# Mixture-of-experts stages: weight rows in 8 KB runs, and the gather of the next pair moved into the current pair

## The chip, the cores and the metric

The kernel runs on one core of a Trainium2 chip. The time is that of one execution on the device, in microseconds (us); the profile is of one such execution. PE is the matrix engine and PEld its loads of the stationary operand; DVE, ACT and POOL are the other compute engines, and SP issues nearly all weight transfers. SBUF is the memory on the core, with 128 partitions, and PSUM holds the sums of PE.

## The reference

A stack of layers on 256 tokens of 1024 features, all in f32. Two of them end in a mixture of 32 experts, and the change concerns these two stages alone:

```python
def moe(x):                                   # x [256, 1024]
    g = softmax(x @ w_rg + b_rg)              # 4 groups, the best one is taken
    e = softmax((x @ w_re + b_re)[group])     # 8 experts in it, the best two
    gates = g_best * e_best / sum(e_best)
    for each expert e, for its tokens xb:
        h = silu(xb @ w_gate[e]) * (xb @ w_up[e])     # [1024, 512] each
        y[tokens] += gate * (h @ w_down[e])           # [512, 1024]
    return y
x = layer_norm(ALPHA * x + moe(x))
```

Every expert is computed in 64 places, whether or not so many tokens chose it; an expert with more tokens is continued in a loop at run time (`more`), which the inputs at hand may leave empty.

## The kernel before

`moe` (L1281 and below) handles the 32 experts as 16 pairs. In a pair, 128 rows of the products are the 64 places of the one expert and the 64 of the other, and PE computes both side by side.

- **Router.** Logits are summed over the eight feature chunks of `X["h"]` and `X["l"]` (L1302, L1303), as the layer norm before it delivers them. DVE finds groups, experts and places. `xt` is x with tokens on partitions, made by 16 transposes.
- **Gather.** `ot` is a 0/1 matrix (tokens by places) for a pair. `xg` is `xt` transposed times `ot`: 16 products (L1455) whose stationary operand is a block of 128 features of `xt`. Each f32 product is two loads and two multiplies on PE, so 32 steps. The results stand in two PSUM tiles of the pool `mp` (tag "m", two buffers, which `ogp`, `htp` and both `yp` use as well, in the order of the code) and are copied to SBUF (L1460).
- **Weights of the places.** `ogt` is `ot` times the gates; it is transposed into `ogp` (L1463) and copied to `og` on ACT.
- **Gate and up.** 64 products into `gps` and `ups` (L1478).
- **Activation.** ACT takes the tanh (L188); DVE makes `t` (L1493, L1494); PE transposes it in four blocks, `htp` (L1497); DVE copies it to `hT` (L1499).
- **Down.** 32 products into two `yp` (L1510), which ACT copies to `y` (L1519). `y` shares one SBUF buffer with `xg` (tag "xy").
- **Combine.** Eight products of `y` and `og` add to the sums `eacc` (L1535). Before pair 0 combines, `residual` (L1437) puts x times ALPHA into these sums, with 16 products of `xt`.

The last pair (`last`) also computes means and high and low parts for the layer norm that follows.

Weights come through `load`: per expert two tiles each of gate, up and down, 1 MiB each, into a ring of 21 tiles (`ORDER`: rooms of several pools) that `next_tile` takes in turn. SP runs ahead of PE; a transfer waits until its tile is free. The rows of a matrix are spread over partitions by

```python
w[k][h * 512:(h + 1) * 512, :].rearrange("(c p) m -> p c m", p=128)   # gate, up: 4 runs of 2 KB a partition
w[2][h * 256:(h + 1) * 256, :].rearrange("(c p) m -> p c m", p=128)   # down: 2 runs of 4 KB a partition
```

`more()` stands behind pair `MOREQ` = 10. Its loop body, which also takes tiles of the ring, is in a branch on a count that DVE computes after pair 1 (`beyond`).

The order of the instructions on an engine is largely that of the code, but the program that builds the kernel may move an instruction that is ready ahead of one that waits. `warm` puts idle products on PE behind an instruction.

Of the kernel before, what the change touches and what calls it, by code (L numbers as in the profile page):

```python
# [10 lines left out]
F32 = mybir.dt.float32  # L11
# [7 lines left out]
D = 1024  # L19
S = 256  # L20
# [11 lines left out]
W1 = 0  # L32
# [15 lines left out]
def tile_stack(ctx: ExitStack, tc: tile.TileContext, a: dict, out: bass.AP):  # L48
# [20 lines left out]
    def after_norm(*ins):  # L69
        """no split but the first few between the operations of a layer norm."""  # L70
# [21 lines left out]
    def project_group(tiles, ws):  # L92
        """up to four chunks at once, (wh, wl, width) each; features outermost, so that it can start on the first."""
        for c in range(KC):
            for i, (wh, wl, n) in enumerate(ws):
                mm3(tiles[i // 2][0:n, i % 2, :], wh[:, c], wl[:, c], X["h"][:, c, :], X["l"][:, c, :],
                    first=(c == 0 and i % 2 == 0), last=(c == KC - 1), skip=True)
        return [tiles[i // 2][:, i % 2, :] for i in range(len(ws))]
# [74 lines left out]
    X = {}  # L173

    def x_tile(key, shape=(128, KC, S), dtype=F32R):
        """the room of a part of x; between its last reader and the next x it takes weights."""
# [13 lines left out]
    def table(name):  # L190
        """the functions' tables, loaded behind the last tanh."""
# [4 lines left out]
    def warm(out, n, after):  # L196
        """the array's clock falls in a pause: idle products, into a sum not in use, keep it up."""
# [5 lines left out]
    def last_chunks(accs, ks, first):  # L203
        """the products of the last chunks, (wh, wl, mh, ml) each, into one output chunk."""
# [7 lines left out]
    def finish(accs, last, scale, g, b, write=None, loaded=False, mean=None, side="right"):  # L212
        """last(c) makes output chunk c of the sum in accs complete; then x = LN(x * ALPHA + acc / scale),
        or LN(acc) where the sum has x in it and its mean is known.

        The variance is taken about the mean of the first
        eighth of the features: the shift from the true mean is at most a few deviations, so the correction
        loses nothing."""
# [99 lines left out]
    def ffn(l, w1, w2, g, b, setup=None):  # L318
        with pool(name="accps", bufs=1, space=PSUM) as aps, pool(name="gups", bufs=2, space=PSUM) as gps, \
# [26 lines left out]
            def gate_up(js):  # L346
                """the hidden chunks js; features outermost, so that it can start on the first of them."""
# [42 lines left out]
    def log1p_exp_neg_abs(pool, x, shape, tag):  # L390
        """log(1 + exp(-|x|)) by the series of atanh."""
# [34 lines left out]
    def bias_tile(pool, h, queue=None, bufs=3):  # L426
        """T[q, k] = rel[bucket(128 + q - k), h], with the mask of the head's kind."""
# [48 lines left out]
    def token_mix(l):  # L476
        w_in, w_gate, w_out = a["w_in"][l], a["w_gate"][l], a["w_out"][l]
        with ExitStack() as st:
# [25 lines left out]
            def split_pair(t0, t1, c0):  # L504
                """stationary columns: 64 of t0, 64 of t1."""
# [19 lines left out]
            def k_pad(ps, kz, i):  # L525
                """a projected pair of keys into two tiles, each with zeros in the other's rows."""
# [10 lines left out]
            def v_tok(ps, v, i):  # L537
                """keys on partitions: v[:, tile, i, :]."""
# [7 lines left out]
            # compressed keys and values  # L546
# [28 lines left out]
            def compress(i, ts):  # L575
                """four products side by side, then their sum."""
# [26 lines left out]
            # compressed keys  # L603
# [23 lines left out]
            # compressed values  # L627
# [15 lines left out]
            # gates of the three branches and the forget gate  # L643
# [15 lines left out]
            # the running sums of the forget gates  # L659
# [9 lines left out]
            # attention over the compressed blocks, all heads at once  # L669
# [29 lines left out]
            def attend(q, kz, bias, sink=None, gate=None):  # L699
                """probabilities of one head, keys on partitions: [k0 x (q0 q1) | k1 x q1]."""  # L700
# [27 lines left out]
            def pv(po, jobs):  # L728
                """jobs[g]: list of (v of tile 0, v of tile 1 or None, probabilities)."""
# [55 lines left out]
            # NSA  # L785
# [17 lines left out]
            # sliding window with sinks  # L803
# [20 lines left out]
            # forgetting attention  # L824
# [79 lines left out]
    def rsqrt_tile(pool, v, eps, n=S):  # L904
        """(v + eps) ** -0.5, refined by a step of Newton's."""
# [9 lines left out]
    def ssd(g, b):  # L915
        w_in, w_out = a["ssd_w_in_2"][0], a["ssd_w_out_2"][0]
        with ExitStack() as st:
# [13 lines left out]
            def conv(ps, c, dst):  # L931
                """causal convolution of four taps, then twice its silu."""
# [9 lines left out]
            # the keys and queries of the states, B and C  # L942
# [6 lines left out]
            # steps, decays and their running sums  # L949
# [47 lines left out]
            def mix(j, xs, csb, y):  # L997
                """the states' sums for two heads."""
# [85 lines left out]
    def dilated(g_, b_):  # L1084
        wq, wo = a["attn_w_qkv_2"][0], a["attn_w_o_2"][0]
        with ExitStack() as st:
# [27 lines left out]
            # sin, with its sign by row, and cos, one where nothing turns  # L1114
# [136 lines left out]
    NE, CAP, HID, NOV = 32, 64, 512, 7  # L1251
    AHEAD = 7
    MOREQ = 10
# [18 lines left out]
    def router_parts(rp, l):  # L1272
        """the router's weights, high and low parts side by side."""
# [5 lines left out]
    def moe(l, g_, b_, rs, write=False):  # L1279
        w_g, w_u, w_d = a["moe_w_gate_2"][l], a["moe_w_up_2"][l], a["moe_w_down_2"][l]  # L1280
        with ExitStack() as st:  # L1281
# [17 lines left out]
            # router  # L1299
            ps = mp.tile([72, S], F32, tag="m", name="lgp")  # L1300
            for c in range(KC):
                nc.tensor.matmul(out=ps, lhsT=rs[:, c, :], rhs=X["h"][:, c, :], start=(c == 0), stop=False, skip_group_check=True)  # L1302
                nc.tensor.matmul(out=ps[0:36], lhsT=rs[:, c, 0:36], rhs=X["l"][:, c, :], start=False, stop=(c == KC - 1), skip_group_check=True)  # L1303
            lf = T([72, S], "lf")
# [4 lines left out]
            warm(accs[0][:, 0, :], W1, x)  # L1309
            # the groups' logits, filled up to eight, then the experts'  # L1310
# [7 lines left out]
            def top(x, name):  # L1318
                """the eight highest logits in order, and where they stand."""
# [8 lines left out]
            # the experts of the other groups far below  # L1328
# [8 lines left out]
            # which experts  # L1337
# [5 lines left out]
            # tokens on partitions  # L1343
# [8 lines left out]
            # the place of each token in its expert's list, -1 if it is in none  # L1352
# [7 lines left out]
            warm(accs[0][:, 0, :], W2, x)  # L1360
# [6 lines left out]
            def weights():  # L1367
                """of the experts chosen."""
# [27 lines left out]
            def beyond():  # L1396
                """blocks of 64 places beyond an expert's first"""
# [33 lines left out]
            def residual():  # L1431
# [296 lines left out]
```

## Time and profile before

| | us |
|---|---|
| median of three runs | 2939.56 |
| lowest and highest | 2938.95, 2942.76 |
| span of the profiled execution, first to last instruction | 2939.3 |
| PE busy | 2802.7 (95%) |
| PE loads busy | 2199.8 (75%) |
| DVE busy | 1421.7 (48%) |
| ACT busy | 1050.9 (36%) |
| POOL busy | 196.5 (7%) |

The profile states no other time of its own for the profiled execution than its span. Shares of busy time are means over stages with different limits: a change in one stage is to be read from that stage. A wait is put down to what ended last before the engine went on. PE's products are pipelined, so that the duration of one contains its drain, and the distance between the starts of two is what one costs in a row of them. The first expert stage lies at about 1700 to 2195 us of the span, the second at about 2425 to 2920.

### The profile page before, as it was taken

The page shows a single profiled execution, that of the slowest core. Times are in us where ns is not written, and L with a number is a line of the kernel's source. Part 1 is how long each engine was busy: PE and PEld are TensorE (multiplying, and loading weights), DVE is VectorE, ACT ScalarE, POOL GpSimd, SP SyncE. Part 2 cuts the span into 40 slices and gives each one's busy share as a digit, 9 for nine tenths or more (in the row PEclk, how much of TensorE's full clock was granted, in tenths as well). Part 3 has the DMA queues.
Part 4 walks back from the last instruction along what each step waited for, and adds up shares of the span by engine and source line. Part 5 has one row for each costly group of instructions (what it writes and reads, how often), then busy time and mean ns, then how long its engine had stood idle before and what let it go on. Part 6 is the DMA issues. An engine that isn't in the chain of part 4 may idle for free. (4 is left out here: it accounts for less than half of the span.)

```text
span 2939.3 us, 46679 instructions
## 1 busy us (share of the span) xinstructions
PE 2802.7 (95%) x19161; PEld 2199.8 (75%) x19161; DVE 1421.7 (48%) x3075; ACT 1050.9 (36%) x1949; POOL 196.5 (7%) x263
## 2 busy tenths in 40 slices
PE   8899999999999999999999999999998989999998
PEld 8798899999999889999989854454448974444454
DVE  5466665755655765665688731111127762111113
ACT  4344555544544454544477510000015530000002
POOL 2102000200201100020100100000001010000000
PEclk9899999999999999999999999999999999999999
DMA  8666454455454745445455699998985479999896
GB/s 223 193 201 158 126 159 138 156 184 185 149 194 137 186 130 167 153 139 193 131 194 180 229 364 393 395 393 323 393 305 169 137 256 356 394 393 393 300 394 230
DMA packets 426793, 697.44 MB, mean 237 GB/s; under 512 B 19460, under 2 KB 238384, under 8 KB 426576
## 3 DMA queue, kind: packets, MB, share of 16 engines
q1 hardware_dynamic: 414976, 677.62, 66.3%
q10 hardware_dynamic: 9296, 11.66, 1.3%
q0 software_dynamic: 2304, 5.15, 1.2%
q8 instruction: 152, 2.49, 0.4%
q14 instruction: 65, 0.53, 0.1%
HBM read 693.25 MB, written 4.27 MB: 237 GB/s over the span
## 5 line engine op out<-in xcount | busy, mean ns | idle before, releaser
L84 DVE TENSOR_TENSOR whl<-w,whl 128x1024 fp32r<-128x1024 f32 x487 | 591.5, 1220 | 349.2 <-ACT whl L83 344.2
L83 ACT ACTIVATE whl<-w 128x1024 fp32r<-128x1024 f32 x487 | 507.3, 1050 | 355.9 <-PE gu L113 105.8
L111 PE MATMUL pp<-xh,whl 128*128 128x256 f32 x1432 | 418.1, 292 | 9.0 <-ACT xh L307 4.0
L112 PE MATMUL pp<-xl,whl 128*128 128x256 f32 x1432 | 418.7, 292 | 1.0 <-DVE xl L308 1.0
L113 PE MATMUL pp<-xh,whl 128*128 128x256 f32 x1432 | 412.8, 288 | 0.4 <-DVE whl L510 0.4
L111 PE MATMUL gu<-xh,whl 128*128 128x256 f32 x1408 | 401.6, 286 | 9.9 <-DVE h L361 7.2
L113 PE MATMUL gu<-xh,whl 128*128 128x256 f32 x1408 | 401.4, 285 | 0.5 <-DVE whl L84 0.5
L112 PE MATMUL gu<-xl,whl 128*128 128x256 f32 x1408 | 401.6, 285 | 0.0
L111 PEld LDWEIGHTS pp<-xh,whl 128*128 128x128 f32 x1432 | 274.6, 192 | 17.4 <-ACT xh L307 5.7
L112 PEld LDWEIGHTS pp<-xl,whl 128*128 128x128 f32 x1432 | 275.0, 192 | 10.0 <-issue 6.9
L111 PEld LDWEIGHTS gu<-xh,whl 128*128 128x128 f32 x1408 | 272.8, 194 | 12.2 <-ACT whl L83 9.4
L113 PEld LDWEIGHTS pp<-xh,whl 128*128 128x128 f32 x1432 | 274.6, 192 | 4.3 <-issue 2.4
L112 PEld LDWEIGHTS gu<-xl,whl 128*128 128x128 f32 x1408 | 273.0, 194 | 0.8 <-DVE xl L308 0.7
L113 PEld LDWEIGHTS gu<-xh,whl 128*128 128x128 f32 x1408 | 272.9, 194 | 0.8 <-DVE whl L84 0.8
L1460 DVE COPY xg<-xgp 128x512 f32<-128x512 f32 x60 | 41.5, 692 | 358.5 <-PE xgp L1455 358.5
L111 PE MATMUL acc<-hhi,whl 128*128 128x256 f32 x704 | 201.7, 287 | 2.4 <-DVE rT L231 2.2
L112 PE MATMUL acc<-hlo,whl 128*128 128x256 f32 x704 | 200.1, 284 | 0.0
L113 PE MATMUL acc<-hhi,whl 128*128 128x256 f32 x704 | 199.1, 284 | 0.0
L1493 DVE SCALAR_TENSOR_TENSOR t<-t,gps 128x512 f32<-128x512 f32 x32 | 22.0, 688 | 324.4 <-ACT t L188 324.4
L1519 ACT ACTIVATE y<-yp 128x512 f32<-128x512 f32 x60 | 35.8, 597 | 347.7 <-PE yp L1510 347.7
L111 PEld LDWEIGHTS acc<-hhi,whl 128*128 128x128 f32 x704 | 135.8, 193 | 5.4 <-DVE rT L231 4.0
L112 PEld LDWEIGHTS acc<-hlo,whl 128*128 128x128 f32 x704 | 135.8, 193 | 0.2
(571 smaller groups left out, 5063.0 us busy)
## 6 DMA issues: line engine op xcount, KB each, us to landing
w<-in_ffn_w_dram SPq DMA_DIRECT2D x130, 1024.0 KB, 5.3
wa<-in_moe_w_up_dram SPq DMA_DIRECT2D x48, 1024.0 KB, 14.2
whl<-in_moe_w_down_dram SPq DMA_DIRECT2D x47, 1024.0 KB, 14.1
wa<-in_moe_w_gate_dram SPq DMA_DIRECT2D x43, 1024.0 KB, 14.2
whl<-in_moe_w_gate_dram SPq DMA_DIRECT2D x39, 1024.0 KB, 14.1
wa<-in_moe_w_down_dram SPq DMA_DIRECT2D x37, 1024.0 KB, 13.4
whl<-in_moe_w_up_dram SPq DMA_DIRECT2D x36, 1024.0 KB, 14.2
w<-in_moe_w_down_dram SPq DMA_DIRECT2D x32, 1024.0 KB, 14.4
```

The source lines that it names most:

```text
L83: after_norm(nc.scalar.activation(out=hi, in_=w, func=AF.Copy), nc.vector.tensor_tensor(out=lo, in0=w, in1=hi.bitcast(F32), op=ALU.subtract))
L84: nc.vector.tensor_tensor(out=lo, in0=w, in1=hi.bitcast(F32), op=ALU.subtract))
L111: nc.tensor.matmul(out=o, lhsT=wh, rhs=xh, start=first, stop=False, skip_group_check=skip)
L112: nc.tensor.matmul(out=o, lhsT=wh, rhs=xl, start=False, stop=False, skip_group_check=skip)
L113: return nc.tensor.matmul(out=o, lhsT=wl, rhs=xh, start=False, stop=last, skip_group_check=skip)
L1460: nc.vector.tensor_copy(out=xg[:, q * 4:q * 4 + 4, 0:P], in_=ps[:, :, 0:P])
L1493: nc.vector.scalar_tensor_tensor(out=t[0:P], in0=t[0:P], scalar=1.0, in1=gps[0:P], op0=ALU.add, op1=ALU.mult)
L1519: nc.scalar.activation(out=y[0:P, hs], in_=yp[0:P], func=AF.Copy)
```

## The change

- Weights: row 4p + c of a gate or up tile and row 2p + c of a down tile now go to partition p, so that a partition's part of a tile is one run of 8 KB.
- To match, the gather takes every fourth feature from `xt` as the columns of a stationary operand, and the transposes of `t` take every second one.
- The gather becomes a function of two halves. Pair 0's runs before the pairs; that of pair q + 1 runs within pair q: its first half behind the tanh in the code, its second half behind the copy of `hT`. The first half's copy to `xg` goes to ACT, the second's to DVE. `xg` has a buffer of its own; `y` becomes two halves in the rooms of `t` and `hT`.
- `ogp` and `og` move behind the gather's second half, except in the last pair.
- The residual moves into the router: eight products of `alphas` and `X["T"]`, two chunks behind the router's, the last two behind the transposes of the logits. The idle products behind the places (`warm`) write to another tile.
- `more()` moves behind the loads of the last pair and takes a tile of the ring for its `xg`.

The core of the diff (comments and docstrings that it also empties are left out):

```diff
 
 ps = mp.tile([72, S], F32, tag="m", name="lgp")
+def residual(c):
+    nc.tensor.matmul(out=accs[c // 2][:, c % 2, :], lhsT=alphas, rhs=X["T"][:, c, :], start=(c % 2 == 0), stop=False,
+                     skip_group_check=True)
 for c in range(KC):
     nc.tensor.matmul(out=ps, lhsT=rs[:, c, :], rhs=X["h"][:, c, :], start=(c == 0), stop=False, skip_group_check=True)
     nc.tensor.matmul(out=ps[0:36], lhsT=rs[:, c, 0:36], rhs=X["l"][:, c, :], start=False, stop=(c == KC - 1), skip_group_check=True)
+    if c >= 2:
+        residual(c - 2)
 lf = T([72, S], "lf")
 nc.scalar.activation(out=lf, in_=ps, func=AF.Identity, bias=rb[:, l:l + 1], scale=1.0)
 pt = mp.tile([128, 2, 72], F32, tag="m", name="lgt")
 for i in range(2):
     x = nc.tensor.transpose(pt[:, i, :], lf[:, i * 128:(i + 1) * 128], ident[0:72, 0:72])
-warm(accs[0][:, 0, :], W1, x)
+for c in (KC - 2, KC - 1):
+    residual(c)
 lg = T([128, 2, 40], "lg")
 nc.vector.memset(lg[:, :, 4:8], -3.0e38)
 lo = T([128, 2, 36], "lo")
...
-warm(accs[0][:, 0, :], W2, x)
+warm(gup.tile([128, HID], F32, tag="u", name="idle")[:, 0:256], W2, x)
...
 
-def residual():
-    if "r" not in done:
-        done["r"] = True
-        for c in range(KC):
-            for i in range(2):
-                x = nc.tensor.matmul(out=accs[c // 2][:, c % 2, i * 128:(i + 1) * 128], lhsT=xt[:, i, c * 128:(c + 1) * 128],
-                                     rhs=alphas, start=(c % 2 == 0 and i == 0), stop=False, skip_group_check=True)
-                tc.add_manual_dep(x.ins, done["up"].ins.name, order, reason="gates first")
-
 done = {}
 
 def first_copy(k):
     return nc.vector.tensor_copy if k == 0 else (lambda out, in_: nc.scalar.activation(out=out, in_=in_, func=AF.Copy))
 
-def run(os, ogs, loads, n, last):
+def gather(os, P, xg):
+    def half(q):
+        ps = mp.tile([128, 4, 128], F32, tag="m", name="xgp")
+        first = "r" not in done
+        for c in range(4):
+            for i in range(2):
+                nc.tensor.matmul(out=ps[:, c, 0:P], lhsT=xt[:, i, q * 512 + c:(q + 1) * 512:4], rhs=os[i],
+                                 start=(i == 0), stop=(i == 1))
+            if first:
+                first_copy(c % 2)(out=xg[:, q * 4 + c, 0:P], in_=ps[:, c, 0:P])
+        if not first:
+            first_copy(1 - q)(out=xg[:, q * 4:q * 4 + 4, 0:P], in_=ps[:, :, 0:P])
+    return [lambda q=q: half(q) for q in range(2)]
+def run(xg, ogs, loads, n, last, then=()):
     P = n * CAP
     wg, wu, wd = loads
-    xg = wk.tile([128, KC, 128], F32, tag="xy", name="xg", bufs=1)
-    for q in range(2):
-        ps = mp.tile([128, 4, 128], F32, tag="m", name="xgp")
-        for c in range(4):
-            for i in range(2):
-                nc.tensor.matmul(out=ps[:, c, 0:P], lhsT=xt[:, i, (q * 4 + c) * 128:(q * 4 + c + 1) * 128], rhs=os[i],
-                                 start=(i == 0), stop=(i == 1))
-            if "r" not in done:
-                first_copy(c % 2)(out=xg[:, q * 4 + c, 0:P], in_=ps[:, c, 0:P])
-        if "r" in done:
-            nc.vector.tensor_copy(out=xg[:, q * 4:q * 4 + 4, 0:P], in_=ps[:, :, 0:P])
-    ogp = mp.tile([128, S], F32, tag="m", name="ogp")
-    for i in range(2):
-        nc.tensor.transpose(ogp[0:P, i * 128:(i + 1) * 128], ogs[i], ident)
-    og = wk.tile([128, S], F32R if last else F32, tag="og", name="og", bufs=1)
-    nc.scalar.activation(out=og[0:P], in_=ogp[0:P], func=AF.Copy, scale=0.5)
+    then = list(then)
     if last:
+        ogp = mp.tile([128, S], F32, tag="m", name="ogp")
+        for i in range(2):
+            nc.tensor.transpose(ogp[0:P, i * 128:(i + 1) * 128], ogs[i], ident)
+        og = wk.tile([128, S], F32R, tag="og", name="og", bufs=1)
+        nc.scalar.activation(out=og, in_=ogp, func=AF.Copy, scale=0.5)
         ogl = wk.tile([128, S], F32R, tag="ogl", name="ogl", bufs=1)
         nc.vector.scalar_tensor_tensor(out=ogl, in0=ogp, scalar=0.5, in1=og.bitcast(F32), op0=ALU.mult, op1=ALU.subtract)
         room = big.tile([128, 2, D], F32, tag="xtok", name="room")
...
     tanh(out=t[0:P], in_=gps[0:P], scale=0.5)
+    if then:
+        then.pop(0)()
     if last:
         table("natural_log_exp_and_others")
     nc.vector.scalar_tensor_tensor(out=t[0:P], in0=t[0:P], scalar=1.0, in1=gps[0:P], op0=ALU.add, op1=ALU.mult)
     nc.vector.tensor_tensor(out=t[0:P], in0=t[0:P], in1=ups[0:P], op=ALU.mult)
     ht = mp.tile([128, 4, 128], F32, tag="m", name="htp")
     for c in range(4):
-        nc.tensor.transpose(ht[:, c, 0:P], t[0:P, c * 128:(c + 1) * 128], ident[0:P, 0:P])
+        nc.tensor.transpose(ht[:, c, 0:P], t[0:P, c // 2 * 256 + c % 2:(c // 2 + 1) * 256:2], ident[0:P, 0:P])
     hT = wk.tile([128, 4, 128], F32, tag="hT", name="hT", bufs=1)
     nc.vector.tensor_copy(out=hT[:, :, 0:P], in_=ht[:, :, 0:P])
+    if then:
+        then.pop(0)()
+    if not last:
+        ogp = mp.tile([128, S], F32, tag="m", name="ogp")
+        for i in range(2):
+            nc.tensor.transpose(ogp[0:P, i * 128:(i + 1) * 128], ogs[i], ident)
+        og = wk.tile([128, S], F32, tag="og", name="og", bufs=1)
+        nc.scalar.activation(out=og[0:P], in_=ogp[0:P], func=AF.Copy, scale=0.5)
     yl = None
     if last:
         y, yl = split_tile([128, D])
-    else:
-        y = wk.tile([128, D], F32, tag="xy", name="y", bufs=1)
     yps = [mp.tile([128, 512], F32, tag="m", name="yp") for hf in range(2)]
     for c0 in range(0, 4, 2):
         for hf, yp in enumerate(yps):
...
+    if not last:
+        ys = [wk.tile([128, 512], F32, tag=k, name="y", bufs=1) for k in ("t", "hT")]
     for hf, yp in enumerate(yps):
         hs = slice(hf * 512, (hf + 1) * 512)
-        nc.scalar.activation(out=y[0:P, hs], in_=yp[0:P], func=AF.Copy)
+        nc.scalar.activation(out=y[0:P, hs] if last else ys[hf][0:P], in_=yp[0:P], func=AF.Copy)
         if last:
             nc.vector.tensor_tensor(out=yl[:, hs], in0=yp, in1=y[:, hs].bitcast(F32), op=ALU.subtract)
     if last:
...
-        nc.tensor.matmul(out=accs[c // 2][:, c % 2, :], lhsT=y[0:P, cs], rhs=og[0:P],
+        nc.tensor.matmul(out=accs[c // 2][:, c % 2, :], lhsT=ys[c // 4][0:P, c % 4 * 128:c % 4 * 128 + 128], rhs=og[0:P],
                          start=False, stop=True, skip_group_check=True)
 
     if last:
         return combine, mean
-    residual()
+    done["r"] = True
     for c in range(KC):
         combine(c)
 
...
         for k, dst in ((0, wg), (1, wu)):
             for e, w in enumerate(ws):
                 t = next_tile([128, 4, HID])
-                x = nc.sync.dma_start(out=t, in_=w[k][h * 512:(h + 1) * 512, :].rearrange("(c p) m -> p c m", p=128))
+                x = nc.sync.dma_start(out=t, in_=w[k][h * 512:(h + 1) * 512, :].rearrange("(p c) m -> p c m", p=128))
                 if turn[0] < len(slots) and "early" in behind:
                     tc.add_manual_dep(x.ins, behind["early"].ins.name, order, reason="the weights at hand first")
                 dst[e].append(t)
     for h in range(2):
         for e, w in enumerate(ws):
             t = next_tile([128, 2, D])
-            nc.sync.dma_start(out=t, in_=w[2][h * 256:(h + 1) * 256, :].rearrange("(c p) m -> p c m", p=128))
+            nc.sync.dma_start(out=t, in_=w[2][h * 256:(h + 1) * 256, :].rearrange("(p c) m -> p c m", p=128))
             wd[e].append(t)
     return wg, wu, wd
 
-def pair(q):
-    ld = load([(w_g[e], w_u[e], w_d[e]) for e in (2 * q, 2 * q + 1)])
-    os, ogs = [], []
+def places(q):
+    os = []
     for i in range(2):
         o = wk.tile([128, 2, CAP], F32, tag=f"ot{i}", name="ot")
         nc.vector.tensor_tensor(out=o, in0=iota[:, 0:CAP].unsqueeze(1).to_broadcast([128, 2, CAP]),
                                 in1=rk[:, i, 2 * q:2 * q + 2].unsqueeze(2).to_broadcast([128, 2, CAP]), op=ALU.is_equal)
         os.append(o)
-    if q == 0:
-        weights()
+    return os
+def weighted(q, os):
+    ogs = []
     for i, o in enumerate(os):
         og = wk.tile([128, 2, CAP], F32, tag=f"ogt{i}", name="ogt", bufs=1)
         nc.vector.tensor_tensor(out=og, in0=o, in1=gt[:, i, 2 * q:2 * q + 2].unsqueeze(2).to_broadcast([128, 2, CAP]), op=ALU.mult)
-        os[i] = o.rearrange("p e s -> p (e s)")
         ogs.append(og.rearrange("p e s -> p (e s)"))
-    return run(os, ogs, ld, 2, q == NE // 2 - 1)
+    return ogs
+def gather_pair(os):
+    xg = wk.tile([128, KC, 128], F32, tag="xg", name="xg", bufs=1)
+    return xg, gather([o.rearrange("p e s -> p (e s)") for o in os], 2 * CAP, xg)
 
 def more():
     total = nc.values_load(ib[0:1, 7:8], min_val=0, max_val=NOV)
...
                 ogs.append(og)
-            run(os, ogs, ld, 1, False)
-
-for q in range(NE // 2):
-    last = pair(q)
+            xg = next_tile([128, KC, 256])
+            for f in gather(os, CAP, xg):
+                f()
+            run(xg, ogs, ld, 1, False)
+
+NP = NE // 2
+for q in range(NP):
+    ld = load([(w_g[e], w_u[e], w_d[e]) for e in (2 * q, 2 * q + 1)])
+    if q == 0:
+        os = places(0)
+        weights()
+        xg, steps = gather_pair(os)
+        for f in steps:
+            f()
+    if q == NP - 1:
+        more()
+    ogs = weighted(q, os)
+    steps = ()
+    if q < NP - 1:
+        os = places(q + 1)
+        hold = {}
+
+        def first_half(os=os, hold=hold):
+            hold["xg"], hold["steps"] = gather_pair(os)
+            hold["steps"][0]()
+
+        steps = (first_half, lambda hold=hold: hold["steps"][1]())
+    last = run(xg, ogs, ld, 2, q == NP - 1, steps)
+    if q < NP - 1:
+        xg = hold["xg"]
     if q == 1:
         beyond()
-    if q == MOREQ:
-        more()
 st4.close()
 ocp = st.enter_context(pool(name="oc", bufs=2))
 o = []
 
 def out_chunk(c):
-    """chunk c of x to where it belongs, tokens on partitions."""
+
     if c % 2 == 0:
         o[:] = [ocp.tile([128, 2, 256], F32, tag="oc", name="oc")]
```

## Rows read from the trace of the kernel before

**Rows 1.** the page's slices: GB/s moved in 40 equal slices of the span
```profile
GB/s 223 193 201 158 126 159 138 156 184 185 149 194 137 186 130 167 153 139 193 131 194 180 229 364 393 395 393 323 393 305 169 137 256 356 394 393 393 300 394 230
```

**Rows 2.** stretches: length, busy by engine (instructions), PEclk, DMA share, GB/s
```profile
1816.00:1836.00 20.00, 19.82 (x108) 10.99 (x110) 2.33 (x7) 1.58 (x3) 0.00 (x0) 1.00 1.05 387
...
1838.00:1848.00 10.00, 8.31 (x42) 2.90 (x40) 2.06 (x3) 0.60 (x1) 0.00 (x0) 1.00 1.03 407
...
2007.00:2020.00 13.00, 13.00 (x78) 8.52 (x76) 1.38 (x2) 1.58 (x3) 0.00 (x0) 1.00 0.06 26
```

**Rows 3.** order of time on DVE: start, duration, instruction; the copies of hT
```profile
1721.41 0.69 DVE L1499 COPY hT<-htp 128x512 f32<-128x512 f32 x1 [0.84 <-PE htp L1497]
...
1753.97 0.69 DVE L1499 COPY hT<-htp 128x512 f32<-128x512 f32 x1 [0.81 <-PE htp L1497]
...
2030.72 0.69 DVE L1499 COPY hT<-htp 128x512 f32<-128x512 f32 x1 [0.81 <-PE htp L1497]
...
2062.06 0.69 DVE L1499 COPY hT<-htp 128x512 f32<-128x512 f32 x1 [0.81 <-PE htp L1497]
...
2751.21 0.69 DVE L1499 COPY hT<-htp 128x512 f32<-128x512 f32 x1 [0.81 <-PE htp L1497]
...
2783.95 0.69 DVE L1499 COPY hT<-htp 128x512 f32<-128x512 f32 x1 [0.81 <-PE htp L1497]
```

**Rows 4.** waits of PE's loads, second stage: us in total, times, longest
```profile
PEld ups L1478 <- DMA whl<-in_moe_w_up_dram: 0.3, 1, 0.3
```

**Rows 5.** order of time on SP and PE, end of the second stage
```profile
2886.41 5.92 SPq L1571 DMA_DIRECT2D wa<-in_moe_w_down_dram  x3
...
2912.47 1.02 PE L1510 MATMUL yp<-wa,hT 128*64 128x512 f32 x3
```

**Rows 6.** the page's DMA issues: count, KB each, us to landing
```profile
whl<-in_moe_w_down_dram SPq DMA_DIRECT2D x47, 1024.0 KB, 14.1
```

**Rows 7.** order of time, one steady pair of the first stage
```profile
1906.96 0.63 PE L1497 MATMUL htp<-ident,t 128*128 128x128 f32 x4 [0.91 <-DVE t L1494]
...
1908.37 0.64 PE L1510 MATMUL yp<-wa,hT 128*64 128x512 f32 x1 [0.78 <-DVE hT L1499]
...
1914.70 0.60 ACT L1519 ACTIVATE y<-yp 128x512 f32<-128x512 f32 x1 [11.41 <-PE yp L1510]
...
1915.44 3.72 PE L1535 MATMUL eacc<-og,y 128*128 128x256 f32 x16
...
1919.00 3.73 PE L1455 MATMUL xgp<-ot,xtok 128*128 128x128 f32 x32
...
1922.88 0.64 PE L1478 MATMUL gps<-wa,xg 128*64 128x512 f32 x1
...
1926.36 3.60 PE L1478 MATMUL ups<-w,xg 128*64 128x512 f32 x16
...
1933.23 3.60 PE L1478 MATMUL ups<-wa,xg 128*64 128x512 f32 x16
...
1937.74 0.63 PE L1497 MATMUL htp<-ident,t 128*128 128x128 f32 x4 [0.91 <-DVE t L1494]
```

**Rows 8.** waits of PE in the router of the second stage
```profile
PE lgp L1302 <- ACT xh L307: 2.1, 3, 0.9
...
PE lgp L1303 <- DVE xl L308: 1.3, 4, 0.7
```

**Rows 9.** groups by line and form: count, busy us, mean ns, idle before
```profile
L1455 PE MATMUL xgp<-ot,xtok 128*128 128x128 f32 x1024 | 121.2, 276 | 1.4 <-DVE xg L1458 0.8 <-PEq L1594 0.6
...
L1455 PEld LDWEIGHTS xgp<-ot,xtok 128*128 128x128 f32 x1024 | 119.7, 192 | 6.0 <-DVE xg L1458 2.8 <-issue 1.3 <-ACT xg L1444 0.2
...
L84 DVE TENSOR_TENSOR whl<-w,whl 128x1024 fp32r<-128x1024 f32 x484 | 590.3, 1225 | 349.2 <-ACT whl L83 344.2
...
L84 DVE TENSOR_TENSOR whl<-w,whl 128x256 fp32r<-128x256 f32 x3 | 1.2, 407 | 0.0
...
L558 DVE TENSOR_TENSOR blk<-pp,pe 64x240 f32<-64x240 f32 x16 | 9.2, 574 | 1.3 <-PE pp L113 1.1
```

More of the change, by code (lines that the diff above doesn't have):

```diff
@@ L31 @@
 WARM = 10
-W1 = 0
 W2 = 4
@@ L1252, in tile_stack @@
     AHEAD = 7
-    MOREQ = 10
     U32 = mybir.dt.uint32
```

## The prediction

> **What bounds the kernel now.** The page's slices come first. In the two expert stages the core reads weights at 393 to 395 GB/s, about twice what the rest of the program asks for [rows 1]; the change works in these stages alone. Stretches of 10 and 20 us then show two limits that nearly coincide: the DMA share stands at 1.03 to 1.05 while gate and up weights (2 KB runs) arrive at 387 GB/s and down weights (4 KB runs) at 407 GB/s, with PE busy beside them [rows 2]. The third view is the order of time on DVE: the copy of `hT`, one per pair, starts every 30.75 us ((2030.72 − 1753.97) / 9) [rows 3]. A pair's weights are 12 MiB, 12.58 MB, which is 31.9 us at 394 GB/s: the transfers are slower than the products by 1.2 us a pair, and live on a lead built up before the first pair. The fourth view, the waits of PE's weight loads, decides which of the two is late: in the whole second stage the largest entry for a transfer is a single wait of 0.3 us [rows 4]. PE's chain sets the time; DMA is close behind.
>
> How close? The last three down transfers are issued by 2886.41 + 5.92 = 2892.3 and a down transfer takes 14.1 us to land, so the last lands at about 2906.4, while the products that need it start at 2912.47 [rows 5, 6]: a spare of 6 us at the end of the stage. In the middle of the first stage DMA stood nearly still for 13 us (26 GB/s) [rows 2]. The code shows why: `more()`, behind pair 10, names six tiles of the ring in a branch that is not taken, and the next loads skip six slots.
>
> **One pair, step by step** [rows 7]. Products start at 1922.88. Gates and ups are 32 steps (two experts side by side); two groups of eight start 6.87 us apart with one group between them (1926.36, 1933.23), so 32 steps are 13.72 us, to 1936.60. Then come two holes: 1.14 us to `htp` (1937.74), with DVE's product `t` in it, and 1.41 from `htp` to `yp` (1908.37 − 1906.96 in the pair before), with the four transposes and DVE's copy `hT`. `yp` to `eacc` is 7.07, `eacc` to `xgp` 3.56, the gather and the two transposes of the weights to the next pair's first product 3.88. The sum is 30.78.
>
> **The change, part by part.**
>
> *The gather moves.* Of its 32 load-and-multiply steps, 0.117 us each (3.73 / 32), 16 now lie ahead of the transposes and 16 behind them; `ogp` follows, then `yp`. With T the end of the ups: the first half's steps end at T + 1.87. `t` was ready by T + 1.14, so `htp` follows at once and its four steps, at the gather's pace, end at T + 2.3. The second half needs the PSUM buffer (of two, "m") that the first half used. The first half's last product ends at 1.87 − 0.117 + 0.276 = T + 2.03 [rows 7, 9]; ACT needs some 0.05 to start, 0.60 for a copy of this size and 0.14 until PE starts (`y`: 1914.70 + 0.60, `eacc` at 1915.44). So the second half starts at T + 2.8, after a new wait of 0.5; its steps end at T + 4.67 and its last product at T + 4.83. DVE's copy takes 0.69, as for `hT`, which is of the same size [rows 3]; with about 0.1 of handing over, `yp`, which takes this buffer, starts at T + 5.61. `ogp` and its copy fit in between. The pair is 13.72 + 5.61 + 7.07 + 3.56 = 29.96 us, 0.79 less than 30.75. That holds for 15 of 16 pairs: the first gather stays exposed, and the last pair gathers for no other. 15 × 0.79 = 11.8 us a stage, 23.7 in both. Bounds: without any handing over PE's own steps would be 3.73 + 0.47 + 0.15 = 4.35 instead of 5.61, 2.05 saved a pair and 60 in all; with hand-overs that cost 0.8 more, nothing is saved.
>
> What is queued behind the new waits: on ACT `og` and the copies of `y`, which come later; on DVE the next pair's places, needed a pair later. `y` in the rooms of `t` and `hT` adds no wait: the transposes that read `t` are long past, and the copy into `hT` starts after the last product that reads it.
>
> *The residual moves* from pair 0 to the router. Pair 0 took 32.56 us from `hT` to `hT`, 1.81 over a steady pair [rows 3]; that goes. In the router PE waits 2.1 + 1.3 = 3.4 us for the norm's chunks [rows 8], room for most of 16 products of 256 columns (3.56 us, as `eacc`). They read `xT` two chunks behind the router, so POOL, which writes it last, has the time. I charge 0.7 for what does not fit ahead of the last router product: 1.1 gained a stage, 2.2 in both. Bounds: 1.8 gained to 1.8 lost a stage (half of 3.56).
>
> *`more()` moves* behind the last pair's loads, so that no load skips slots. Pair 11 took 2783.95 − 2751.21 = 32.74 us in the second stage and 31.34 in the first [rows 3], 2.0 and 0.6 over. The 0.6 now stands before the last pair, with the branch; 1.4 goes, at the least nothing, at the most 2.6. For dilated attention, which follows the first stage, two raw tiles come free some 10 us later, with the last pair's down products; its products wait for the norm at the end of the stage, which comes later still, so nothing is charged; if that cover failed it would be those 10 us, once.
>
> *8 KB runs.* From 2 to 4 KB runs the rate rose from 387 to 407 GB/s [rows 2]; 8 KB runs are not in the trace. If a run costs a fixed time and a time per byte, 8 KB give about 418 GB/s, 30.1 us a pair (an estimate from these two rows); below, no gain, 31.9 us; a loss cannot be excluded either, and is a rival. In the first two cases the time gains nothing, because PE, which sets it, asks for a pair each 29.96 us, and at the old rate the spare at the stage's end is 6 + 13 (the pause gone) − 12 (the faster PE) = 7 us. So this part is costed at zero; its cover is that spare.
>
> *The step of four.* Each f32 column of the gather's stationary operand is now 16 bytes from the next (8 in `htp`). Today's loads of the gather read columns side by side, 192 ns each, overlapped to 0.117 us [rows 7, 9], and no row shows a stepped load. The nearest is on DVE: `blk` (L558), which steps in what it reads and writes, takes 574 ns for 240 elements, where L84 gives 407 for 256 and 1225 for 1024, 1.07 ns an element plus 134; the stepped one is (574 − 134) / 240 = 1.83, 1.7 times as much [rows 9]. At the other end the step costs nothing; a gain is excluded, since as many columns are read as before. I take zero, because `blk` steps by 64 and 128 bytes, in PSUM too and on another engine; the other end is the first rival.
>
> [...]
>
> *Sum:* 2939.3 − 23.7 − 2.2 − 1.4 = 2912.0, against the span of the profiled execution, 0.3 below the median of the runs. Forecast **2912 us**, its own range 2898 to 2924.
>
> **The rivals.**
>
> *Stepped loads cost (slower).* If the ratio of `blk` holds, a gather step is 0.201 us instead of 0.117. The first half ends at T + 3.2, the second starts at T + 4.1 and ends at T + 7.3, `yp` starts at T + 8.15; the pair is 32.50, 1.75 over today's. 15 × 1.75 + 2.7 for the exposed first gather = 29 a stage, 58 in both, less 3.6 of the other parts: 2994. With loads twice as long it would be 33.5 a pair, 3025. It decides where half a gather grows by 0.4 us, at a step of 0.142. For it: in the gather a load follows a load with nothing to spare. Against: the nearest row is far away.
>
> *DMA becomes the bound (slower).* If 8 KB runs came 5% slower, a stage's transfers (16 × 31.9 = 510 us) would last 25 longer against a spare of 7: 2912 + 2 × 18 = 2948. It decides at 4%: 20 us of 510, the spare and what the other parts gain. Against it: the rise from 2 to 4 KB.
>
> *The change does not do what it says.* The holes are filled, but the two hand-overs of the one PSUM buffer eat what is gained: within 6 us of 2939.
>
> **How the numbers follow.** Forecast 0.58, stepped loads 0.30, DMA 0.06, no gain 0.06. The range 2896 to 3005 leaves out a little at the fast end and the upper half of the stepped case: it holds 0.55 + 0.15 + 0.06 + 0.05 = 0.81. A measurement of this kernel tells 0.2%, 6 us, from no change: faster 0.59, same 0.05, slower 0.36.
>
> **What would show it.** Right: copies of `hT` some 30.0 us apart; no hole before `htp`, 0.5 before the gather's second half and again before `yp`; gather steps still 0.117 apart; no wait for weights. Wrong: gather loads longer than 192 ns or spaced wider, pairs of 32 us or more; or PE waiting for transfers late in a stage, at fewer GB/s than 394.

## The result, and the profile after

The changed kernel takes **3107.5 us** (median of four runs, 3102.1 to 3112.1) where the kernel before took 2940.7 beside it: 1.057 times as long, with an interval of 1.0555 to 1.0586. The forecast was 2912, its range ended at 3005. The change loses 167 us, and the time is also above what the rival "stepped loads cost" gave (2994, and 3025 with loads twice as long). The profiled execution spans 3104.9 us.

The page of the changed kernel, PE and the GB/s of the 40 slices:

```profile
PE 2992.0 (96%) x19129; PEld 2337.2 (75%) x19129; DVE 1402.3 (45%) x3051; ACT 1070.8 (34%) x1985; POOL 196.2 (6%) x263
...
GB/s 211 209 178 174 125 166 137 163 188 139 203 177 162 129 163 144 149 196 132 192 168 271 327 375 348 344 339 336 247 113 153 215 267 375 363 337 344 344 335 49
```

The full slices of the expert stages now show 327 to 375 GB/s, where most showed 393 to 395 [rows 1]. That alone does not say whether transfers or products are late. The order of time on DVE, the copies of `hT`, shows where the time lies (start, duration; the bracket is the idle time ahead and what ended it):

```profile
1798.23 0.69 DVE L1503 COPY hT<-htp 128x512 f32<-128x512 f32 x1 [3.71 <-PE htp L1501]
1832.47 0.69 DVE L1503 COPY hT<-htp 128x512 f32<-128x512 f32 x1 [3.71 <-PE htp L1501]
...
1976.47 0.69 DVE L1503 COPY hT<-htp 128x512 f32<-128x512 f32 x1 [0.84 <-PE htp L1501]
2013.55 0.69 DVE L1503 COPY hT<-htp 128x512 f32<-128x512 f32 x1 [0.84 <-PE htp L1501]
```

There are two kinds of pairs: 34.24 us early in a stage, 37.08 later (16 such intervals in both stages, and two more of 37.5), against 30.75 [rows 3]. The idle time ahead of the copy differs too, 3.71 and 0.84, so the instructions around it stand in another order. The loads of the gather in the changed kernel (busy us, mean ns; idle before):

```profile
L1449 PEld LDWEIGHTS xgp<-ot,xtok 128*128 128x128 f32 x1024 | 247.6, 327 | 70.5 <-issue 47.1 <-PE ups L1480 8.1 <-ACT xg L1440 7.3
```

A load of the gather takes 327 ns where it took 192 [rows 9]; 1024 of them keep PEld busy for 247.6 us, 0.242 a step against the 0.117 of before. Now the early pair on PE, ups already done (the view ends at 1836, within the second half):

```profile
1827.96 4.00 PE L1449 MATMUL xgp<-ot,xtok 128*128 128x128 f32 x16
1831.80 0.63 PE L1501 MATMUL htp<-ident,t 128*128 128x128 f32 x4
1832.65 3.53 PE L1449 MATMUL xgp<-ot,xtok 128*128 128x128 f32 x14 [0.22 <-ACT xg L1440]
```

This is the order that the prediction reckoned with: half a gather behind the ups, `htp` without a hole, 0.22 of waiting, the second half; only each half takes 3.84 us (1827.96 to 1831.80). The late pair:

```profile
1954.48 1.07 PE L1480 MATMUL gps<-wa,xg 128*64 128x512 f32 x2
1955.48 0.73 PE L1449 MATMUL xgp<-ot,xtok 128*128 128x128 f32 x2
1956.15 0.64 PE L1480 MATMUL gps<-w,xg 128*64 128x512 f32 x1
1956.16 0.64 PE L1480 MATMUL gps<-wa,xg 128*64 128x512 f32 x1
...
1958.78 1.02 PE L1480 MATMUL gps<-w,xg 128*64 128x512 f32 x2
1959.73 1.20 PE L1449 MATMUL xgp<-ot,xtok 128*128 128x128 f32 x4
1960.86 1.07 PE L1480 MATMUL ups<-w,xg 128*64 128x512 f32 x2
1961.86 2.60 PE L1449 MATMUL xgp<-ot,xtok 128*128 128x128 f32 x10
...
1975.68 0.75 PE L1501 MATMUL htp<-ident,t 128*128 128x128 f32 x4 [0.78 <-DVE t L1498]
1976.27 3.88 PE L1449 MATMUL xgp<-ot,xtok 128*128 128x128 f32 x16
```

Here the build has moved the first half of the gather forward, in pieces of 2, 4 and 10 steps among the gates and ups. Around a piece the two experts get out of step: two `gps` or `ups` of one expert run alone (1.02 to 1.07 us, one behind the other), where the products of two experts otherwise start together. And `htp` waits for `t` again, as before the change: the hole that the gather was to fill is open.

### The profile page after: what moved, and what is told of

Read it like the earlier page. It is cut to its first block, busy times and chain, and to the rows that moved or that the text cites. A ratio compares the mean times of both kernels' runs of the same rounds, so it can differ in the third digit from the quotient of the medians.

```text
span 3104.9 us, 46603 instructions
## 1 busy us (share of the span) xinstructions
PE 2992.0 (96%) x19129; PEld 2337.2 (75%) x19129; DVE 1402.3 (45%) x3051; ACT 1070.8 (34%) x1985; POOL 196.2 (6%) x263
## 5 line engine op out<-in xcount | busy, mean ns | idle before, releaser
L1449 PEld LDWEIGHTS xgp<-ot,xtok 128*128 128x128 f32 x1024 | 247.6, 327 | 70.5 <-issue 47.1
L1449 PE MATMUL xgp<-ot,xtok 128*128 128x128 f32 x1024 | 266.5, 406 | 2.2 <-ACT xg L1440 2.2
L187 ACT ACTIVATE t<-gps 128x512 f32<-128x512 f32 x32 | 19.1, 597 | 523.4 <-PE gps L1480 523.4
```

The costliest lines, as they stand in the source:

```text
L187: last_tanh.append(nc.scalar.activation(out=out, in_=in_, func=AF.Tanh, **kw))
L1449: nc.tensor.matmul(out=ps[:, c, 0:P], lhsT=xt[:, i, q * 512 + c:(q + 1) * 512:4], rhs=os[i], start=(i == 0), stop=(i == 1))
```

## The experiments

Each is timed beside the kernel before; ratios are to it, with their interval. "Step" is the theory that the stepped loads are the loss; "order" that the pieces are; "transfers" that the 8 KB runs are.

**xt_side: the step taken away.**

```diff
-nc.scalar.activation(out=xt[:, i, q * 512:(q + 1) * 512], in_=pt.rearrange("p c t -> p (c t)"), func=AF.Copy)
+nc.scalar.activation(out=xt[:, i, q * 512:(q + 1) * 512].rearrange("a (c p) -> a c p", c=4),
+                     in_=pt.rearrange("p c t -> p (c t)").rearrange("a (p c) -> a c p", c=4), func=AF.Copy)
...
-lhsT=xt[:, i, q * 512 + c:(q + 1) * 512:4]
+lhsT=xt[:, i, (q * 4 + c) * 128:(q * 4 + c + 1) * 128]
```

> The changed kernel, but xt is stored with its features reordered (by the copies out of PSUM that write it), so that the gather reads its stationary columns side by side again; 8 KB runs, order of the products and htp's step of two stay. Theory step (the gather's stepped loads pace it at 0.24 us a step instead of 0.117): 32 gathers x 32 steps x 0.122 us = 125 us come back, 3107 to 2982, gather steps 0.12 apart, weight loads near 192 ns. Theory order (the loss is the pieces into which the gather's first half is cut among gates and ups, and the hole left before htp): the pieces stay, so 3107, at best 3090. Theory transfers (8 KB runs hold PE up): 3107.

Measured: 2980.3 us, 1.0146 [1.0129, 1.0163]. 127 us came back, as the step theory said. Its loads of the gather:

```profile
L1450 PEld LDWEIGHTS xgp<-ot,xtok 128*128 128x128 f32 x1024 | 123.4, 192 | 70.2 <-issue 47.1 <-PE ups L1481 8.1 <-ACT xg L1441 7.3
```

192 ns and 0.120 a step again, with the idle times of the pieces unchanged (47.1, 8.1, 7.3). The kernel is still slower than before, by the other part.

**pin_half: the pieces taken away, the step left.** Every product `x` of the gather is held behind the last ups product ahead of it (`done["up"]`); the lines added:

```diff
+if "up" in done:
+    tc.add_manual_dep(x.ins, done["up"].ins.name, order, reason="ups first")
```

> The changed kernel, with the gather held behind the last ups product of the pair, so that it is no longer cut into pieces among gates and ups; loads stepped as in the change. Theory step alone: 3107, pairs keep their length. Theory order as a second part of the loss: the pairs of 37.07 us become pairs of 34.23; there are about 19 of them, 19 x 2.84 = 54 us, 3053. Theory order alone (the step is harmless): 2920 to 2941.

Measured: 3050.3 us, 1.0376 [1.0359, 1.0393]; 57 us back. Two copies of `hT`, and the pair on PE:

```profile
1970.67 0.69 DVE L1505 COPY hT<-htp 128x512 f32<-128x512 f32 x1 [3.67 <-PE htp L1503]
...
2004.65 0.69 DVE L1505 COPY hT<-htp 128x512 f32<-128x512 f32 x1 [3.67 <-PE htp L1503]
```

```profile
1986.26 3.65 PE L1482 MATMUL gps<-whl,xg 128*64 128x512 f32 x16
...
2000.14 4.00 PE L1449 MATMUL xgp<-ot,xtok 128*128 128x128 f32 x16
2003.98 0.63 PE L1503 MATMUL htp<-ident,t 128*128 128x128 f32 x4
2004.83 4.00 PE L1449 MATMUL xgp<-ot,xtok 128*128 128x128 f32 x16 [0.22 <-ACT xg L1440]
```

Gates and ups take 13.88 us (1986.26 to 2000.14). In the cut pair of the changed kernel they take 1954.48 to 1974.90 (`htp` less its wait of 0.78), 20.42; without the 16 steps of 0.24 in them 16.6, 2.7 more. From the end of the ups to the second half it is 1.37 there (1976.27), here 4.69 (2004.83), of which the first half is 3.84: 0.85. So the hole before `htp` costs 0.5, and with the 2.7 that is, to 0.1, the 3.1 us between 37.08 and the 33.98 of this kernel.

**side_pin: both.**

> Both edits: xt reordered so that the gather reads side by side, and the gather held behind the ups. If step and order together are the whole loss, 3107 - 125 - 54 = 2928, and pairs of about 30.0 us, as forecast (2912), with no hole before htp. If the 8 KB runs hold PE up, above 2941, with waits of the weight loads for DMA.

Measured: 2923.7 us, 0.9950 [0.9932, 0.9969], faster than before. The two parts add: 127 + 57 = 184, and 3107.5 − 2923.7 = 183.8. A steady pair, and the start of the next (2006.16 to 2036.24 is 30.08):

```profile
2006.16 3.65 PE L1483 MATMUL gps<-wa,xg 128*64 128x512 f32 x16
...
2020.04 2.05 PE L1450 MATMUL xgp<-ot,xtok 128*128 128x128 f32 x16
2021.93 0.64 PE L1504 MATMUL htp<-ident,t 128*128 128x128 f32 x4
2022.78 2.05 PE L1450 MATMUL xgp<-ot,xtok 128*128 128x128 f32 x16 [0.21 <-ACT xg L1441]
2024.67 0.38 PE L1512 MATMUL ogp<-ident,ogt 128*128 128x128 f32 x2
2025.53 4.08 PE L1523 MATMUL yp<-w,hT 128*64 128x512 f32 x17 [0.47 <-ACT og L1514]
...
2032.59 3.72 PE L1550 MATMUL eacc<-og,y 128*128 128x256 f32 x16
2036.24 3.65 PE L1483 MATMUL gps<-wa,xg 128*64 128x512 f32 x16
```

The first pairs of a stage take 30.33 us: there the build puts two `gps` of the next pair ahead of `yp` (1814.19 and 1814.74).

**layout_only: the kernel before with the 8 KB runs and the steps, nothing else.** The edits are the four `rearrange` and slice lines of the change.

> The kernel before, with the weights in 8 KB runs and the stepped reads that they ask for (gather by four, htp by two); nothing pipelined, nothing moved. Theory step: 32 pairs x (32 x 0.122 + 4 x 0.077) us = 135 us more, 2941 to 3076, pairs of 35 us. Theory order: 2941, as no gather is cut there. Theory transfers: above 2941, with waits for DMA.

Measured: 3071.5 us, 1.0448 [1.0431, 1.0466]: 132 us, with no pipelining and no pieces. Two of its copies of `hT`, 34.60 us apart, 3.9 more than before:

```profile
1795.90 0.69 DVE L1499 COPY hT<-htp 128x512 f32<-128x512 f32 x1 [0.90 <-PE htp L1497]
1830.50 0.69 DVE L1499 COPY hT<-htp 128x512 f32<-128x512 f32 x1 [0.90 <-PE htp L1497]
```

Seven of the 30 intervals are 1.5 to 1.8 us longer than that makes them. The interval ahead of these two copies (36.30 us) is one, and it differs from theirs in the granted clock (length, busy by engine, PEclk, DMA share, GB/s):

```profile
1759.60:1795.90 36.30, 34.61 (x150) 18.35 (x150) 10.14 (x29) 2.17 (x4) 0.00 (x0) 0.95 0.85 348
1795.90:1830.50 34.60, 32.91 (x150) 17.95 (x150) 4.34 (x9) 2.17 (x4) 0.00 (x0) 1.00 0.89 365
```

The longer interval has a mean granted clock of 0.95, the one behind it 1.00. Together the seven are some 12 us of the profiled execution, which took 3076.9, and are not the price of the step, which is the 3.9 us a pair, some 124 in 32 pairs. In the kernel before all 30 intervals have a mean granted clock of 1.00; why it is lower here is open.

**step2_pin and step8_pin: the size of the step.** As pin_half, with the rows of gate and up laid out so that the gather steps by two (4 KB runs) or by eight (8 KB runs still). The patterns of the weights' transfers, abridged; the slices of the gather follow them:

```diff
-w[k][h * 512:(h + 1) * 512, :].rearrange("(p c) m -> p c m", p=128)            # step 4
+w[k][h * 512:(h + 1) * 512, :].rearrange("(a p c) m -> p a c m", a=2, c=2)     # step 2
+w[k].rearrange("(p h c) m -> h p c m", h=2, c=4)[h]                            # step 8
```

> The changed kernel with the gather held behind the ups, gate and up weights in 4 KB runs instead of 8, so that the gather's stationary operand is read with a step of two elements instead of four. [...] Theory that any step costs the same: as with four, 0.24 us a step, 3050. Theory that the price goes with the step's bytes: 0.18 us a step, 2987. The transposes htp, at a step of two, grew from 140 to 207 ns a load, which speaks for a price at two.

> The same with a step of eight elements (8 KB runs still, a partition's eight features split between the two halves of a weight). [...] Theory that the price goes with the step's bytes: 0.48 us a step, 32 x 32 x 0.24 = 246 us more, 3296.

Measured: 2930.5 us (0.9964 [0.9952, 0.9976]) at two, 3052.8 (1.0379 [1.0362, 1.0395]) at eight. The loads of the gather, at two and at eight:

```profile
L1449 PEld LDWEIGHTS xgp<-ot,xtok 128*128 128x128 f32 x1024 | 127.4, 197 | 47.5 <-issue 18.7 <-ACT xg L1440 14.7 <-PE ups L1482 7.3
```

```profile
L1449 PEld LDWEIGHTS xgp<-ot,xtok 128*128 128x128 f32 x1024 | 249.6, 334 | 47.7 <-issue 18.7 <-ACT xg L1440 14.8 <-PE ups L1482 7.3
```

Per step 0.124 at two (127.4 / 1024), 0.244 at eight (249.6 / 1024), beside 0.118 at one (1.89 / 16 from the first half to `htp` in side_pin) and 0.240 at four (3.84 / 16 in pin_half). Over these four the price doesn't grow with the step's bytes: it jumps between 8 and 16 bytes. What makes it jump no run shows.

**pipe_pin: weights in the runs of before, no step at all, pipelined and pinned.**

> The kernel with both repairs (side by side, gather held behind the ups), but with the weights in the runs of before (2 and 4 KB), so that no reordering of xt and no step is needed at all: the pipelining and the moves alone. The prediction costed the 8 KB runs at zero, covered by a spare of 7 us at the end of a stage: then 2924, as with 8 KB runs, and hardly a wait for DMA. Rival (the longer runs are what lets PE run at 30.1 us a pair): at 394 GB/s a pair is 31.9 us, 1.8 longer, and without any spare a stage would lose up to 25 us, 2924 to 2974, with waits of gps or ups for DMA late in each stage.

Measured: 2924.1 us, 0.9944 [0.9931, 0.9958], as side_pin. The stretch from 1900 to 2000 us of pipe_pin and then of side_pin (busy by engine, PEclk, DMA share, GB/s):

```profile
1900.00:2000.00 100.00, 97.11 (x507) 48.08 (x507) 12.88 (x30) 9.30 (x17) 0.00 (x0) 1.00 1.04 394
```

```profile
1900.00:2000.00 100.00, 97.26 (x510) 48.81 (x511) 13.41 (x31) 9.29 (x17) 0.00 (x0) 1.00 1.01 419
```

The 8 KB runs do move 419 GB/s instead of 394, and no pair is shorter for it: no single wait of PE's loads for a weight is longer than 0.3 us in either.

**side_whole: the second pair's gather copied in halves.** The first copies of side_pin on DVE:

```profile
1717.17 0.69 DVE L1506 COPY hT<-htp 128x512 f32<-128x512 f32 x1 [1.04 <-PE htp L1504]
1718.89 0.67 DVE L1455 COPY xg<-xgp 128x128 f32<-128x128 f32 x2 [1.02 <-PE xgp L1450]
...
1751.14 0.69 DVE L1506 COPY hT<-htp 128x512 f32<-128x512 f32 x1 [1.77 <-PE htp L1504]
```

```diff
-first = "r" not in done
+first = "up" not in done
```

> Both repairs, and the gather of the second pair copied out in halves like all later ones (in the change it goes chunk by chunk, as it runs before the flag that says that the first pair is through). Its trace shows 33.97 us from hT to hT in the first interval of each stage where the next ones have 30.33. Theory: the chunk-wise copies are that 3.64, 2 x 3.64 = 7 us come back, 2924 to 2917. Rival (it is the first pair's other work): 2924, first interval still 34.

Measured: 2918.9 us, 0.9924 [0.9912, 0.9936]; the first interval is 30.40 us.

**best8 and best_old: `ogp` ahead of the gather.** The transposes `ogp` and their copy are moved to just behind the last ups product; best8 is otherwise side_whole, best_old has the runs of before.

> The kernel with both repairs and whole copies, and the two transposes ogp moved from behind the gather's second half to between the last ups product and the gather's first half. In the run before, products stood still for 0.87 us between the second half's last load and yp, waiting for the copies of ogp and of the gather's second half, which hold the two PSUM buffers. Theory (that is a hand-over, not work): yp's first buffer is then the one that hT was copied from, long free; ogp costs 0.26 us on the other side, 0.6 us a pair come back, 30.09 to 29.5, 30 x 0.6 = 18 us, 2919 to 2901. Rival (PE is so fast now that transfers, 12.58 MB a pair, 426 GB/s, become the bound): 2919 or near it, with waits of gps and ups for DMA.

> The same with the weights in the runs of before (2 and 4 KB; no step, no reordering). At 394 GB/s a pair's weights take 31.9 us against 29.5 of products: a stage falls behind by 16 x 2.4 = 38 us, about the lead that the kernel before lived on (16 x 1.2 + 6 + 13 = 38). Theory (runs of 8 KB begin to pay only here, if at all): 2901 to 2910, with some waits for DMA late in the stages. Rival (length of the runs is worth nothing here): as the kernel with 8 KB runs.

Measured: 2902.8 us (0.9866 [0.9851, 0.9881]) and 2902.1 (0.9868 [0.9853, 0.9883]): both beat the kernel before by 38 us. The pair of best8:

```profile
2016.53 0.44 PE L1499 MATMUL ogp<-ident,ogt 128*128 128x128 f32 x2
2016.80 1.95 PE L1450 MATMUL xgp<-ot,xtok 128*128 128x128 f32 x16
2018.59 0.64 PE L1511 MATMUL htp<-ident,t 128*128 128x128 f32 x4
2019.44 2.05 PE L1450 MATMUL xgp<-ot,xtok 128*128 128x128 f32 x16 [0.21 <-ACT xg L1441]
2021.42 4.08 PE L1524 MATMUL yp<-w,hT 128*64 128x512 f32 x17
```

`yp` starts 4.89 us behind the ups instead of 5.49, and the pair is 29.50. The last 80 us of the first stage, best8 and then best_old:

```profile
2100.00:2180.00 80.00, 77.92 (x390) 38.00 (x387) 15.92 (x33) 10.93 (x21) 0.00 (x0) 1.00 0.60 238
```

```profile
2100.00:2180.00 80.00, 77.85 (x390) 37.62 (x387) 15.60 (x32) 10.76 (x20) 0.00 (x0) 1.00 0.98 365
```

With the old runs the transfers go on to the end of the stage (0.98) where those of 8 KB have slowed down (0.60). Still no wait of PE's loads for a weight is longer than 0.3 us in either: the lead suffices, and the longer runs have still bought nothing.

**more_11 and router_res: the two moves.** more_11 is side_whole with `more()` behind pair 11's loads; router_res is the kernel before with the residual's products in the router.

> The kernel with both repairs and whole copies, but more() behind the loads of pair 11 instead of those of the last pair, so that the loads skip six slots of the ring in the middle of a stage again, as in the kernel before. The prediction gave its move 1.4 us in the second stage, at the most 2.6, at the least nothing: 2919 to 2922, one interval in the middle of each stage longer by 0.6 to 2, and a pause of the transfers of some 13 us.

> The kernel before with one edit: the residual's products stand in the router as in the change (16 of 256 columns, between the router's), not behind the first pair's. The prediction: pair 0 is shorter by 1.8 us, the router longer by 0.7, 2.2 us less in both stages, 2941 to 2939. Rival (they hold the router up for their whole length): 3.56 longer, 2941 to 2945.

Measured: more_11 2920.1 us, 0.9934 [0.9921, 0.9948], no difference from side_whole that can be told. The pause of the transfers is back:

```profile
2020.00:2030.00 10.00, 9.31 (x58) 5.36 (x59) 1.38 (x2) 0.98 (x2) 0.00 (x0) 1.00 0.01 2
```

It delays nothing: the last five intervals of the stage sum to 151.42 us, in side_whole to 151.25. router_res: 2939.1 us, 0.9996 [0.9987, 1.0005], no difference. Pair 0 is 30.77 us instead of 32.56 [rows 3], as reckoned, but the way from the router's first product to the first `hT` [rows 3] is 39.99 instead of 37.35 (the first line is from the kernel before, the others from router_res, the last a group of waits: us in total, times, longest):

```profile
1684.06 0.34 PE L1302 MATMUL lgp<-xh,rs 128*72 128x256 f32 x1
```

```profile
1680.84 0.34 PE L1306 MATMUL lgp<-xh,rs 128*72 128x256 f32 x1
```

```profile
1720.83 0.69 DVE L1496 COPY hT<-htp 128x512 f32<-128x512 f32 x1 [0.75 <-PE htp L1494]
```

```profile
PE eacc L1302 <- POOL xT L310: 2.0, 5, 0.6
```

The residual's products wait for POOL. The products of the places (`rkp`) come 1.5 us later behind the router's first product than before (14.36 instead of 12.83). Another 1.1 is lost from there to the first gather (4.05 instead of 2.96): from the first of the eight idle products there to the gather it is 2.94 us (1696.31 to 1699.25) instead of 1.81 (1698.04 to 1699.85). The second stage loses as much (40.03 instead of 37.34).

## Why the prediction was wrong

**The step of four: the step that failed.** The prediction took zero, because the nearest row, `blk` [rows 9], was far away, and gave the rival 0.30. That distance was a reason to doubt 0.201 us a step, and none for zero. Measured are 0.240 us a step (pin_half) instead of 0.117, 127 us in all (xt_side). In the kernel before it is 132 (layout_only): some 124 by the length of its pairs, and some 12 in seven longer intervals of the profiled execution, the one shown at a granted clock of 0.95. The rival was right that stepped loads cost, and its upper end (loads twice as long) was nearer than the `blk` ratio of 1.7. Beside 0.118 us at a step of one (side_pin), a step of two costs 5% more (0.124, step2_pin), and steps of four and eight about twice as much (0.240, pin_half; 0.244, step8_pin).

**The order: a loss that stood in no case.** The prediction placed the first half behind the ups because the code does, although the build may move an instruction that is ready. In the later pairs the build had it earlier, in pieces, and the filled hole was open again: 57 us (pin_half). The later pairs of xt_side show it without the step: 33.19 us, 3.11 more than those of side_pin. The rival with loads twice as long gave 3025, from pairs of 33.5 us; with the order that it reckoned with the time is 3050, from pairs of 33.98 and the longer first interval below. The rest up to 3107.5 is the order.

**The gather's move** was right where its conditions held. In side_pin `htp` follows the ups by 1.89 us (reckoned 1.87), the second half by 2.74 (2.8), `yp` by 5.49 (5.61), and the pair is 30.08 (29.96): 0.67 saved, not 0.79. Gates and ups take 13.88 (13.72) and `eacc` 3.65 (3.56), so that it is close partly because small errors cancel. What it missed is that the second pair's gather runs before the flag `r` is set and so is copied chunk by chunk, 3.6 us a stage; side_whole takes that back.

**8 KB runs: zero was right**, for the reason given: 419 GB/s came (the estimate was 418), and the spare covered the old runs even at 29.5 us a pair. The rival "DMA becomes the bound" is out.

**The residual** was mis-sized: 1.79 gained in pair 0, but 2.6 lost ahead of it instead of 0.7, so nothing or a little less than nothing instead of 2.2 gained. The prediction held that POOL has the time two chunks behind; PE waits 2.0 us for it (router_res). **`more()`**: nothing instead of 1.4; the pause was hidden by the lead. The 1.4 was also misread, for pair 11 of the second stage lost it in the kernel before at this wait:

```profile
2783.28 0.63 PE L1497 MATMUL htp<-ident,t 128*128 128x128 f32 x4 [2.28 <-DVE t L1494]
```

It is 0.91 in a steady pair [rows 7]. Gate products stood last there (to 2780.95), and tanh (2781.03) and `t` (2781.66) came behind them, so that the loss came by the order of the products. No wait for a transfer is longer than 0.3 us in that stage [rows 4].

Together: 2940.7 + 127 (step) + 57 (order) − 17 (pipelining and moves: side_pin less 2940.7) = 3107.7, against 3107.5. What stays open is why the build cuts the gather in the later pairs and not in the first few of a stage, and why seven intervals of layout_only are longer, the one shown at a granted clock of 0.95.

## What to carry to other kernels

A layout that lengthens transfers moves a step to whoever reads the tile, or the operand that goes with it. Before it is costed at nothing, ask whether the reader is on the path and how far apart its neighbours come to lie (here a step took 0.118 us at 4 bytes, 0.124 at 8 and 0.240 at 16). In this kernel a reordering in a copy that was made anyway (xt_side) removed the step, and 127 us with it; best8, which has that reordering, takes 2902.8 us, and best_old, which does without, 2902.1. Work that is meant to fill a hole has to be held in it: the place in the code was not the place in the stream, and here the pieces among products that run two side by side cost 2.7 us a pair, more than the hole. Before a longer time is put down to an edit, its granted clock is to be read too (0.95 in an interval of layout_only that is 1.7 us longer than the next). And here, with the transfers hidden, faster ones were worth nothing: 2923.7 us at 419 GB/s (side_pin), 2924.1 at 394 (pipe_pin).

## What was not expected of the hardware

PE's f32 loads of 128 columns, back to back with their products, go at 0.118, 0.124, 0.240 and 0.244 us a step when the columns are 4, 8, 16 and 32 bytes apart: over these four one jump, no slope. The loads of `htp`, at 8 bytes, show a longer duration (205 ns in side_whole, 142 in pipe_pin), and a steady pair is 30.08 to 30.09 us in both: the longer loads, beside waits, cost nothing there.
